# Layer 1's attention in a hybrid diffusion backbone: preparation of a pair of heads merged with the scores of the pair before, and a second bank for transposed scores

## The chip, the cores and the metric

The program runs on 1 core of one Trainium2 chip. The metric is the device time of one execution in microseconds (us), as the median of several. Instructions are written for five engines: TensorE (PE in the profile, its weight loads PEld), VectorE (DVE), ScalarE (ACT), GpSimd (POOL) and SyncE (SP, which issues the transfers). Each engine takes the instructions of its own queue in order.

## What is computed

The reference runs two layers over 512 latent tokens (`x`) and 256 context tokens (`ctx`), width 1024. In each layer one projection feeds three groups of heads whose outputs are put side by side and projected back:

- a bidirectional RWKV-7 scan (6 heads of 64),
- latent attention (6 heads; 64 values without and 32 with an axial rotation per head),
- an order-2 Hyena long convolution (256 channels).

Then comes a PEER feed-forward stage over 16384 single-neuron experts. Context tokens read context alone, latent tokens read latents and context. In the last layer only latents are wanted, so attention of the context there makes keys and values only. The part that is changed is this:

```python
q = rms_norm(q, q_gain)
k = rms_norm(k, k_gain)
...
q = concat([q[..., :64], apply_axial_rope(q[..., 64:], rope)])
k = concat([k[..., :64], apply_axial_rope(k[..., 64:], rope)])
...
s = einsum('bqhd,bkhd->bhqk', q, k) * (96 ** -0.5)
pr = softmax(s, axis=-1)
y = einsum('bhqk,bkhd->bqhd', pr, v)
```

## The kernel before

`layer0` (L484) and `layer1` (L540) hold the mixing stages; `ffn` (L1511) the PEER stages. Inside a mixing stage several generators run as tracks: the scan (`rwkv`, L779), Hyena (`hyena_filters` L1249, `hyena` L1338, and in layer 0 after it the modulation of layer 1, `mods` L386), and attention with the projections around it (`mla` L1105, `mixed` L735). Each generator yields numbers, its costs, and `weave` (L336) always goes on with the track whose sum is lowest; `scaled` multiplies a track's costs by a factor (0.42 for the scan in layer 0, 0.8 for that of the latents in layer 1, 0.05 for its context part there, 3.5 for the modulation, 1 for attention). A track that yields a condition (`after`) waits for a mark of another one. The order in which the instructions come out of the weave is their priority: the scheduler of the framework walks it with a model of the engines and puts on each engine's queue the earliest instruction whose inputs and buffers it thinks ready. `merge` (L848) is a small weave inside one track: it runs several generators side by side and yields on only what the slowest of them has advanced, so that two tracks of 46 and 22 units cost 46.

`mla` works for a stream b (0 context, 1 latents) with T tokens in nt tiles of 128. After the norms and V (L1145 to L1148) it goes over three pairs of heads, `g3`:

- Preparation. For keys (g = 1) and then queries (g = 0): products into "mm" (L1163, L1166), copies into `x` by ScalarE (L1164, L1167), squares and sums (L1175, L1176), a yield of 4, an inverse root on VectorE, the gain on GpSimd (L1181), the rotation on VectorE (L1190 to L1193), the scale on GpSimd (L1194), then per head nt transposes into "tr" (L1198), a copy into `kTl` or `qT` (L1200) and a yield of 2. A pair costs 2 x (4 + 2 x 2) = 16 units.
- Scores. Per head, for each tile of queries, products of the scores into "mm" and their maximum by VectorE (L1211); for latents 8 of them, then a yield of 5. The maxima go through "tr" into row 96 of `qT` (L1217, L1218), so that the next products are the transposed scores less the maximum. For each of 6 tiles of keys (2 for the context): the transposed scores into "tr" (L1223), the exponential into `PT` (L1225), the product with V into another "mm" bank (L1227), a yield of 2. Then the reciprocal of the sum (L1231), a wait for Hyena's mark, the product into the mixing tile `zl` (L1233), a yield of 1. A latent head costs 5 + 6 x 2 + 1 = 18 units.

`kTl` and `qT` have one buffer each, `PT` (shared with `sx`, `sq` and `rc`) three. PSUM has eight banks: `ps` (L274) gives two each for "mm", "rw" and "ch", one each for "tr" and "hy". Hyena uses "hy", the scan "rw" and "ch".

In layer 0 attention of the context comes first (78 units), then, once the scan of the context is done, its output projection (24), then attention of the latents, then, after the first mark of the modulation, `mixed` for the latents. The scan is 9 groups of at most 41 units and a last chain of 25, times 0.42: 165.5. In layer 1 attention begins with 27 units of projection for the context and 24 for its keys; the scan is 143 x 0.05 = 7 and then (6 x 41 + 25) x 0.8 = 217. `mixed(1, 1)` (L582) comes after the weave; its first step splits the eight mixing tiles (L748, L749), and the products need all of them.

## Time and profile before

| | us |
|---|---|
| median of 3 runs | 5449.75 |
| lowest and highest | 5433.88, 5454.05 |
| the profiled execution | 5464.84 |
| its span, first to last instruction | 5463.1 |
| TensorE busy | 4928.4 (90%) |
| VectorE busy | 3849.6 (70%) |
| ScalarE busy | 1918.5 (35%) |
| GpSimd busy | 1241.3 (23%) |

The profile is one execution. Times in the rows are microseconds from the start of the span. A busy TensorE is not one at its peak: matmuls overlap and their ends are modelled. L272 is the line of the helper that issues every matmul, so TensorE's rows are told apart by their tiles: `tr<-qT,kTl` are transposed scores, `mm<-PT,Vl` the product with V, `mm<-kTl,qT` the scores for the maxima, `ch<-...` and `rw<-...` the scan, `hy<-...` Hyena, `ch<-wl,silr` the modulation. A matmul of fp32 shows as two instructions.

### The profile page before, as it was taken

How to read it: one execution, taken by the hardware profiler on the slowest of the kernel's cores; microseconds unless marked ns; L12 is line 12 of the kernel's file. 1: busy time of each engine (PE TensorE's matmuls, PEld its weight loads, DVE VectorE, ACT ScalarE, POOL GpSimd, SP SyncE). 2: the span in 40 equal slices, each digit the busy share in tenths (PEclk: the TensorE clock that was granted, in tenths of full speed). 3: DMA queues.
4: the chain of work that ended last, by engine and by line, in shares of the span. 5: the costliest groups of instructions: out<-in, count | busy, mean ns of one | idle time of the engine just before them, and what ended most of it. 6: DMA issues, size and time to landing. Idle time of an engine off the chain costs nothing. (4 is left out here: it accounts for less than half of the span.)

```text
span 5463.1 us, 76042 instructions
## 1 busy us (share of the span) xinstructions
PE 4928.4 (90%) x28693; PEld 3745.5 (69%) x28693; DVE 3849.6 (70%) x8277; ACT 1918.5 (35%) x3438; POOL 1241.3 (23%) x933
## 2 busy tenths in 40 slices
PE   7987998889989999999999678888889889999998
PEld 4765676547644588887878456656657667888887
DVE  6356666656896488887888875656646985777776
ACT  5322222443254333333333232222223454444442
POOL 2322212221200122222222363211122321111110
PEclk9977899899999999999999889777899999999999
DMA  6300121342365788888888764200022668888885
GB/s 207 103 22 31 51 86 55 113 151 71 109 187 162 240 326 316 330 323 311 318 325 303 274 238 153 77 1 1 1 74 82 196 191 295 324 322 312 321 320 206
DMA packets 395517, 1028.18 MB, mean 188 GB/s; under 512 B 31780, under 2 KB 198981, under 8 KB 339597
## 3 DMA queue, kind: packets, MB, share of 16 engines
q1 hardware_dynamic: 339852, 620.65, 34.0%
q0 software_dynamic: 55296, 402.68, 19.6%
q8 instruction: 225, 3.69, 0.3%
q14 instruction: 144, 1.17, 0.1%
HBM read 920.19 MB, written 103.02 MB: 187 GB/s over the span
## 5 line engine op out<-in xcount | busy, mean ns | idle before, releaser
L203 POOL DMA_INDIRECT row<-in_uv,idx x384 | 531.8, 1385 | 1860.8 <-DVE acc L241 1586.7
L659 ACT ACTIVATE wh<-w 128x1024 fp32r<-128x1024 f32 (+1 forms) x557 | 571.0, 1027 | 1049.5 <-PE mm L272 461.7
L272 PE MATMUL mm<-hlo,wh 128*128 128x512 f32 (+2 forms) x2408 | 877.0, 368 | 30.7 <-DVE zl L688 7.5
L272 PE MATMUL mm<-hhi,wh 128*128 128x512 f32 (+2 forms) x2408 | 866.8, 364 | 0.0
L660 DVE TENSOR_TENSOR wl<-w,wh 128x1024 fp32r<-128x1024 f32 x424 | 516.3, 1221 | 255.0 <-ACT wh L659 252.1
L272 PE MATMUL mm<-hhi,wl 128*128 128x512 f32 (+2 forms) x2408 | 531.5, 361 | 1.7 <-POOL wl L660 1.7
L272 PEld LDWEIGHTS mm<-hlo,wh 128*128 128x128 f32 x2408 | 461.2, 192 | 104.4 <-issue 18.4
L241 DVE SCALAR_TENSOR_TENSOR acc<-row,act,acc 128x1024 f32<-128x1024 f32 x381 | 496.5, 1303 | 35.3 <-ACT act L237 34.6
L272 PEld LDWEIGHTS mm<-hhi,wh 128*128 128x128 f32 x2408 | 461.5, 192 | 61.8 <-issue 3.3
L219 DVE SCALAR_TENSOR_TENSOR row<-row,xk 128x1024 f32<-128x1024 f32 x384 | 480.3, 1251 | 16.5 <-DMA row<-in_uv,idx 16.3
L272 PE MATMUL mm<-row,wh 128*128 128x512 f32 (+1 forms) x1056 | 455.5, 574 | 29.9 <-DMA wh<-in_uT 25.1
L272 PEld LDWEIGHTS mm<-hhi,wl 128*128 128x128 f32 x2408 | 425.9, 189 | 56.6 <-issue 3.8
L660 POOL TENSOR_TENSOR wl<-w,wh 128x1024 fp32r<-128x1024 f32 (+1 forms) x133 | 291.4, 2198 | 670.0 <-ACT wh L659 405.3
L272 PEld LDWEIGHTS mm<-row,wh 128*128 128x128 f32 x1056 | 195.3, 195 | 211.2 <-issue 165.4
L236 ACT ACTIVATE act<-act 128x1 f32<-128x1 f32 x384 | 75.7, 197 | 498.6 <-DVE row L219 498.3
L1779 ACT ACTIVATE stage<-ch 128x512 f32<-128x512 f32 x224 | 218.2, 1101 | 62.6 <-PE ch L272 59.8
L1546 ACT ACTIVATE g<-mm 128x512 f32<-128x512 f32 (+1 forms) x256 | 137.6, 538 | 232.3 <-PE mm L272 197.2
L272 PE MATMUL rw<-wh,cl 128*128 128x512 f32 x512 | 201.5, 394 | 6.5 <-DVE cl L1614 3.5
L272 PE MATMUL rw<-wl,ch 128*128 128x512 f32 x512 | 200.5, 392 | 0.0
L272 PE MATMUL rw<-wh,ch 128*128 128x512 f32 x512 | 199.9, 390 | 0.0
L272 PE MATMUL ch<-wh,cl 128*128 128x512 f32 x512 | 199.6, 390 | 0.0
L272 PE MATMUL ch<-wh,ch 128*128 128x512 f32 x512 | 199.4, 389 | 0.0
(542 smaller groups left out, 10206.0 us busy)
## 6 DMA issues: line engine op xcount, KB each, us to landing
w<-in_uv SPq DMA_DIRECT2D x256, 512.0 KB
w<-in_uT SPq DMA_DIRECT2D x190, 512.0 KB
Wd<-stage SPq DMA_DIRECT2D x28, 2048.0 KB
w<-in_mod_w SPq DMA_DIRECT2D x192, 256.0 KB
wh<-in_uT SPq DMA_DIRECT2D x66, 512.0 KB
W<-Wd SPq DMA_DIRECT2D x32, 1024.0 KB
W<-Wd SPq DMA_DIRECT2D x32, 768.0 KB
w<-in_wq SPq DMA_DIRECT2D x32, 512.0 KB
```

The lines of the kernel that those rows point to most:

```text
L203: self.nc.gpsimd.indirect_dma_start(out=row, out_offset=None, in_=self.k.io[f"uv{self.li}"], in_offset=bass.IndirectOffsetOnAxis(ap=self.t ...
L219: nc.vector.scalar_tensor_tensor(row[:, 0:1024], row[:, 0:1024], 1.0, self.x, op0=OP.mult, op1=OP.mult, accum_out=act)
L236: nc.scalar.activation(act, act, AF.Gelu)
L241: nc.vector.scalar_tensor_tensor(self.acc, row[:, 1024:], act, self.acc, op0=OP.mult, op1=OP.add)
L272: self.nc.tensor.matmul(out, lhsT, rhs, start=start, stop=stop, skip_group_check=True)
L659: self.nc.scalar.activation(wh[:, s], w, AF.Copy)
L660: eng.tensor_tensor(wl[:, s], w, wh[:, s].bitcast(F32), op=OP.subtract)
L1546: nc.scalar.activation(g, p[:, 0:ND], AF.Gelu)
L1779: nc.scalar.activation(stage[:, :, u:u + 4].rearrange("p a t -> p t a"), p, AF.Copy, scale=1 / GS)
```

## The change

The body of the loop over pairs is cut into two generators, `prep(g3)` and `attend(g3)`. Before the loop `prep(0)` runs alone; then, for each pair, `attend(g3)` and `prep(g3 + 1)` run merged in layer 1, one after the other in layer 0. In layer 1 `kTl` and `qT` have two buffers. Every second tile of transposed scores goes into the bank "hy" instead of "tr", in either layer, if Hyena of the latents has set its last mark at that point of the program. There are new yields, in either layer: 3 after the scale on GpSimd; 4 after the second and the fourth tile of score maxima of a latent head; and 2 instead of 5 after the last. A latent pair's preparation so costs 22 units and a latent head 23; a context pair's preparation 22 (11 in layer 1, where only keys are made), a context head 5 as before.

```diff
-            for g3 in range(3):
+            def prep(g3):
+
                 if b:
-                    kTl = ap.tile([97, 2, T], F32, name="kTl")
+                    kTl = ap.tile([97, 2, T], F32, name="kTl", bufs=1 + li)
                     nc.gpsimd.memset(kTl[96:97], 1.0)
-                qT = ap.tile([97, 2, T], F32, name="qT") if full else None
+                qT = ap.tile([97, 2, T], F32, name="qT", bufs=1 + li) if full else None
+                made[g3] = kTl if b else None, qT
                 for g in (1, 0):
...
                     nc.gpsimd.tensor_tensor(x2, x2, r[:, :, None].to_broadcast([128, n, 96]), op=OP.mult)
+                    yield 3
                     for h in range(2):
...
                         yield 2
-                if not full:
-                    continue
+
+            def attend(g3):
+                kTl, qT = made[g3]
                 for h in range(2):
...
                             nc.vector.tensor_reduce(mx[:, i, z:z + 1], p, axis=AX.X, op=OP.max)
-                    yield 5 if b else 2
+                        if b and i % 2:
+                            yield 4
+                    yield 2
...
                     for n, kt in enumerate(kts):
-                        p = self.ps("tr")[:, :T]
+                        p = self.ps("hy" if n % 2 and ("hy", li, 1, 1) in self.marks else "tr")[:, :T]
...
                     yield 1
+
+            made = {}
+            yield from prep(0)
+            for g3 in range(3):
+                tracks = ([attend(g3)] if full else []) + ([prep(g3 + 1)] if g3 < 2 else [])
+                yield from self.merge(*tracks) if li else itertools.chain(*tracks)
```

## Rows read from the trace of the kernel before

**Rows 1.** The page, part 2: TensorE and its granted clock in 40 slices
```profile
PE   7987998889989999999999678888889889999998
...
PEclk9977899899999999999999889777899999999999
```

**Rows 2.** Windows: length, PE, PEld, DVE, ACT, POOL busy (instructions), PEclk, DMA share, GB/s
```profile
777.00:1042.00 265.00, 231.99 (x2338) 167.31 (x2336) 185.23 (x479) 78.43 (x155) 65.96 (x50) 0.88 0.22 73
1042.00:1195.00 153.00, 134.13 (x459) 60.12 (x459) 91.78 (x179) 74.74 (x138) 30.98 (x24) 0.90 0.40 121
...
3573.00:4033.00 460.00, 382.53 (x3740) 268.69 (x3738) 290.16 (x803) 123.09 (x246) 60.36 (x48) 0.80 0.01 1
4033.00:4061.00 28.00, 20.83 (x44) 8.40 (x44) 5.33 (x4) 6.69 (x10) 4.67 (x2) 0.74 0.23 75
```

**Rows 3.** Timeline of VectorE at layer 1's end: start, duration, instruction, idle before
```profile
4033.34 0.69 DVE L1102 TENSOR_TENSOR zl<-rw,g 128x512 f32<-128x512 f32 x1 [7.69 <-PE rw L272]
4036.41 0.69 DVE L749 TENSOR_TENSOR mlo<-zl,mhi 128x512 fp32r<-128x512 f32 x1 [2.38 <-ACT mhi L748]
...
4060.40 0.69 DVE L1233 TENSOR_TENSOR zl<-mm,rc 64x512 f32<-64x512 f32 x1
```

**Rows 4.** Timeline of TensorE there: steps of a head, first product of the projection
```profile
4011.37 1.12 PE L272 MATMUL mm<-PT,Vl 128*128 128x512 f32 x2 [0.31 <-ACT PT L1225]
4012.33 1.02 PE L272 MATMUL tr<-qT,kTc 97*128 97x512 f32 x2
4013.19 1.02 PE L272 MATMUL mm<-kTl,qT 96*128 96x512 f32 x2
...
4061.24 0.76 PE L272 MATMUL mm<-mlo,wh 128*128 128x512 f32 x1 [4.26 <-DVE zl L1233]
```

**Rows 5.** Timeline of VectorE at the end of layer 0's scan and of its attention
```profile
1036.45 0.41 DVE L1211 TENSOR_REDUCE mx<-mm 128x1 f32<-128x256 f32 x1
...
1042.09 0.69 DVE L1102 TENSOR_TENSOR zl<-rw,g 128x512 f32<-128x512 f32 x1 [3.11 <-PE rw L272]
...
1193.75 0.69 DVE L1233 TENSOR_TENSOR zl<-mm,rc 64x512 f32<-64x512 f32 x1
```

**Rows 6.** Timeline of ScalarE in layer 1: exponentials and copies into qT
```profile
3741.54 0.60 ACT L1225 ACTIVATE PT<-tr 128x512 f32<-128x512 f32 x1 [2.85 <-PE tr L272]
...
3785.37 0.68 ACT L1200 ACTIVATE qT<-tr,qkc 96x512 f32<-96x512 f32 x1 [1.63 <-PE tr L1198]
...
3906.88 0.60 ACT L1225 ACTIVATE PT<-tr 128x512 f32<-128x512 f32 x1
...
3975.66 0.67 ACT L1200 ACTIVATE qT<-tr,qkc 96x512 f32<-96x512 f32 x1
...
4052.47 0.60 ACT L1225 ACTIVATE PT<-tr 128x512 f32<-128x512 f32 x1 [2.14 <-PE tr L272]
4055.20 0.60 ACT L1225 ACTIVATE PT<-tr 128x512 f32<-128x512 f32 x1 [2.14 <-PE tr L272]
```

**Rows 7.** Timeline of ScalarE in layer 0 after the scan
```profile
1098.59 0.60 ACT L1225 ACTIVATE PT<-tr 128x512 f32<-128x512 f32 x1 [0.84 <-PE tr L272]
...
1129.70 0.68 ACT L1200 ACTIVATE qT<-tr,qkc 96x512 f32<-96x512 f32 x1 [0.58 <-PE tr L1198]
...
1155.69 0.60 ACT L1225 ACTIVATE PT<-tr 128x512 f32<-128x512 f32 x1 [1.22 <-PE tr L272]
1158.42 0.60 ACT L1225 ACTIVATE PT<-tr 128x512 f32<-128x512 f32 x1 [2.14 <-PE tr L272]
...
1187.09 0.60 ACT L1225 ACTIVATE PT<-tr 128x512 f32<-128x512 f32 x1 [1.15 <-PE tr L272]
```

**Rows 8.** Windows, tile tr, then tile mm: length, PE, PEld, DVE, ACT busy
```profile
1042.00:1195.00 153.00, 33.98 (x96) 14.28 (x96) 0.00 (x0) 19.38 (x32) 0.90 0.40 121
...
1042.00:1195.00 153.00, 60.70 (x143) 25.60 (x144) 32.31 (x38) 3.00 (x8) 0.90 0.40 121
```

## The prediction

> **What bounds the kernel now.** I read the page first. Its row of TensorE in 40 slices is nearly full, and shows where it is less so: eights in slices 7 to 9 and 25 to 30, the latter with sevens in the row of the granted clock [rows 1]. Those lie in the two mixing stages, of layer 0 and of layer 1, where attention, the RWKV scan and the Hyena convolution share the engines; the dense PEER stages between them are full and the change doesn't touch them. So I cut the mixing stages into windows. In layer 1 from 3573 (the first preparation of latent heads) to 4033 us, TensorE is busy for 382.5 of 460 us at a granted clock of 0.80, and in the last 28 us, to 4061, for 20.8 at 0.74; the DMA engines are idle. In layer 0, 777 to 1042 us is shared with the scan (232 of 265 busy) and 1042 to 1195 is attention beside the modulation of layer 1 (134 of 153) [rows 2]. Neither stage is full, none waits for memory: what ends last there is a chain.
>
> Which chain, the VectorE timeline tells. In layer 1 the scan's last output is written at 4033.3, the last head of attention at 4060.4, and between them VectorE does almost nothing [rows 3]. TensorE's first products of the output projection that need that head start at 4061.2, after 4.3 us of waiting for it [rows 4]. So attention ends layer 1's mixing, 27 us after everything else. In layer 0 it is the same, only more: the scan's last output is at 1042.1, the last head at 1193.8 [rows 5], and the projection follows at once. Attention's own length is therefore worth time in both layers, and the scan's length is worth time as the point from which attention stands alone.
>
> Attention's length has two visible parts. One is serial preparation: in layer 1 the last exponential of pair 0 is at 3741.5 and the last copy into qT of pair 1 at 3785.4, 44 us; from pair 1 to pair 2 it is 3906.9 to 3975.7, 69 us [rows 6]. The other is the single bank for transposed scores: at the end the exponentials come every 2.73 us, 0.60 of it work and 2.14 waiting for TensorE [rows 6], and in layer 0's lone stretch it is the same 2.73 [rows 7]. TensorE's share of such a step is one product of scores and one with V: 4011.37 to 4012.33 and 4012.33 to 4013.19, together 1.82 us [rows 4].
>
> **The change part by part.** No instruction is added or taken away, and no transfer, so SP's queue is passed by nothing; the extra buffers of kTl and qT in layer 1 are memory alone. What changes is order, and one bank.
>
> *Layer 1, preparation beside scores.* Preparation of pairs 1 and 2 leaves the chain, 44 and 69 us as it stands. That isn't the gain, because the scan goes on meanwhile: if attention stops being last, the scan's end at 4033.3 is, and the most that can be won with the scan unmoved is 4061.2 - 4037 (its copy and split of that tile follow in 4 us: the VectorE row at 4036.4 [rows 3]) = 24 us. Does attention get there? The yields are the clock by which the tracks are woven. Before, attention of layer 1 takes 27 + 24 units for the context and then 3 x (16 + 2 x 18) = 156, so it is due at 207; the scan is due at 7 + 0.8 x 271 = 224. Attention was due 17 units before the scan and came 27 us after it: it was late by its chain, not by its order. After, a preparation is 22 and a head 23 units, the context ends at 60, and the merge takes 22 + 3 x 46 = 160: due at 220, still before the scan. With the chain shorter by 113 us and the due time later by 13 of 217 scan units (13/217 of 460 us, 28 us), attention should come within some us of the scan. Against it stands work: the last head's products now run before 4033 instead of after. TensorE's 20.8 us of the last 28 [rows 2] have to fit into 77 idle us of the 460; I let 6 of them push the scan out. Sum -24 + 6 = **-18 us**; ends: 0 if attention is still last, and -40 if a denser order also moves the scan up (a fifth of those 77 idle us, an estimate).
>
> *Shared banks.* In the merge the next preparation draws on the bank "tr" and the two "mm" banks that the scores use, and the three PT buffers. Four transposed copies of 0.68 us a pair [rows 6] and their transposes sit between steps of the present pair. They cost attention's chain perhaps 4 x 2 us a pair; it has 113 us to give, so nothing, and 16 us if that cover is gone. The preparation's GpSimd work moves past the scan's in that queue, and GpSimd is busy for 60 of the 460 us [rows 2]: nothing. The second bank is Hyena's; in either layer its mark says that Hyena is done, so nobody queues behind it.
>
> *Layer 0, the yields.* Here the order within attention stays, but its clock doesn't: 156 units become 204, and the context's 78 become 96, because the new yields stand outside the test on the layer. The scan is due at 0.42 x 394 = 165.5 in both. Before, attention stands there at 165.5 - 102 = 63 of its 156 units: two heads done and most of preparation 1. After, at 165.5 - 120 = 45 of 204: one head. So one head and one preparation are moved behind the scan, where attention is alone. Alone a head takes 28.7 us (last exponential 1158.4 to 1187.1) and a preparation 31.8 (1098.6 to the end of 1129.7 + 0.68) [rows 7]: 60.5. The traced order runs ahead of the woven one (head 2's maxima are already being reduced at 1036 us [rows 5], due at 170 units and the scan's end at 165.5), so I take three quarters, +45. The scan gains what it no longer shares: attention's tiles take 34.0 + 60.7 = 94.7 us of TensorE for four heads and one preparation [rows 8]; counting a preparation as half a head, head and preparation are 32, three quarters of it 24, at 88% busy about -20 us. Ends: 0, if TensorE fills idle time with attention as before, and +45 with nothing moved up.
>
> *The second bank.* In layer 1 the Hyena mark is due at 60, before all six heads; in layer 0 at 164, after head 0, so for five heads. In layer 1 it helps to reach the bound that is taken above and counts once. In layer 0 each step may fall from 2.73 to 1.82: 0.9 x 5 steps x 5 heads = -22; I take **-17**, since the modulation's products stand in the same queue; ends 0 and -22. The Trainium skill, page "TensorE: Matmul & The Clock Gate", section "HAM oscillation — how this bites in real kernels", reports a kernel where adding PSUM double-buffering gave no further gain once its loop order was right. By that this term would be 0 and layer 0's sum +25; the 2.14 us of waiting before exponentials in this trace speak against it.
>
> *Layer 0's other queues.* The modulation now has its units before attention's end (318 against 324, before 318 against 258), so it comes earlier in every queue; TensorE's products for it already ran mostly before 1195. I cost it at nothing; if it takes precedence over attention it is in the end of +45.
>
> **Sum.** Layer 0: +45 - 20 - 17 = +8. Layer 1: -18. Together -10 us. The profiled execution is 5464.84 us for a span of 5463.1, 15 us over the median of 5449.75, itself within 5433.9 to 5454.1. Against the span 5453, against the median **5440 us**. About 27 us, 0.5%, is what a measurement of this kernel can tell from no change, and the forecast is inside it.
>
> **The rivals.**
> *A, layer 1 gives more.* Three tracks instead of two fill TensorE's gaps, the scan's end moves up too, and layer 0's order turns out to matter little because ready work is issued when the engine is free. Layer 1 -35, layer 0 between -10 and 0: about 5410. For it: 77 idle us and the clock of 0.80 in layer 1, which is a mean of stretches at 1.2 and at 2.4 GHz. Against it: the scan's own chain isn't shortened by anything.
> *B, slower.* Layer 0's attention is pushed behind the scan and stays there. Place: the stretch from the scan's last output to the last head, 152 us now. Price: +60 with -26 back from the scan, and nothing from the second bank, since steps are already interleaved with products of the modulation in TensorE's one queue; +34 in layer 0, -5 in layer 1: about 5479. It decides once more than a head's length is moved without the step falling below 2.5 us. The skill's sentence above is on its side; the trace, with 2.14 us of idle ScalarE a step, against it.
> *C, the change doesn't do what it says in layer 1.* Preparation and scores fight over "tr" and "mm"; attention still ends 20 us after the scan. Layer 1 0 to -5, layer 0 +8: about 5455.
>
> **How the numbers follow.** Forecast 0.50; A 0.26; B 0.14; C 0.10. Forecast and C lie within 27 us, A beyond it on the one side, B on the other: faster 0.26, same 0.60, slower 0.14. Range: from a little under A, 5400, to B, 5478; the forecast's own, with the ends of its terms, is 5415 to 5470.
>
> **What would show it.** Right in layer 1: the preparation's kTl and qT copies of the next pair lie between exponentials of the present one, exponentials come under 2.2 us apart at the end, and the last head is written within 10 us of the scan's last output. Right in layer 0: the scan's last output moves up by 10 to 30 us, the stretch from it to the last head grows from 152 us to 165 to 190, steps in it fall towards 2 us. The forecast is wrong if layer 0's stretch grows with the scan's end unmoved (B), or if the scan in layer 1 itself ends over 15 us sooner (A), or if attention is still over 15 us late there (C).

## The result: slower by half a per cent, and the profile after

The changed kernel takes **5490.4 us** (median of 8 runs, 5467.86 to 5505.14) against 5452.14 for the kernel before (8 runs, 5433.88 to 5470.19): ratio **1.0066 [1.0044, 1.0089]**. A second measurement, below, gives 1.0049 [1.0031, 1.0068]. The change is slower: by 38 us in the first measurement and by 27 in the second; 5440 was forecast.

The profiled execution took 5477.02 us, its span is 5475.3, only 12.2 over the one before, since the profiled execution before lies over its kernel's median (5464.84 against 5452.14) and this one under its own. Going by marks that both traces have, these 12.2 us are: +26.0 up to the first top-16 maximum (L1437 before, L1449 after) of layer 0's PEER stage (1286.3 to 1312.4); -12.5 in that stage, which the change doesn't touch (2150.4 to 2137.9 until layer 1's first Hyena output; in the profiles of this study it takes 2138 to 2165); -2.6 in layer 1's mixing (630.1 to 627.5 until its first projection output at L762); +1.3 behind it. By this profile the loss is layer 0's, and layer 1 gives nothing; runs of either layer alone, below, bear it out.

The page, part 2, of the changed kernel:

```profile
PE   7987898889988999999999778889889889999998
...
PEclk9976898899999999999999889867789999999999
```

Against [rows 1] the digits hardly move: layer 1's begin 7, 7, 8 for 6, 7, 8, with a 9 among its eights, over a clock that now shows a 6; slice 5, the end of the context's part in layer 0, has an 8 for a 9, and so has slice 13, outside both stages. No stage has become full, and none much emptier; digits are too coarse for half a per cent. The two stages in windows (columns as in [rows 2]); first layer 0 from its first values of the context (L1148) to the end of the context's scan and on to the first top-16 maximum, then its lone stretch, then layer 1:

```profile
319.00:616.00 297.00, 241.97 (x2027) 179.44 (x2027) 203.64 (x554) 76.40 (x161) 71.98 (x82) 0.72 0.11 36
616.00:1312.00 696.00, 609.68 (x4708) 402.49 (x4707) 427.07 (x1005) 232.87 (x432) 149.22 (x115) 0.89 0.28 90
...
1032.00:1222.00 190.00, 162.18 (x548) 75.28 (x546) 114.14 (x260) 89.58 (x169) 39.11 (x30) 0.87 0.35 107
3450.00:4078.00 628.00, 524.68 (x4849) 379.75 (x4849) 383.80 (x1054) 170.53 (x337) 99.03 (x81) 0.78 0.07 23
3582.00:4064.00 482.00, 410.30 (x3770) 286.69 (x3770) 293.84 (x820) 131.22 (x261) 59.31 (x47) 0.78 0.02 6
4051.00:4064.00 13.00, 5.05 (x24) 3.26 (x24) 3.52 (x12) 0.63 (x1) 3.78 (x3) 0.50 0.46 161
```

The same three stretches of the kernel before, which the prediction hadn't cut so:

```profile
318.00:609.00 291.00, 234.43 (x2011) 176.13 (x2010) 201.84 (x551) 73.81 (x159) 73.09 (x82) 0.74 0.10 33
609.00:1286.00 677.00, 602.17 (x4695) 396.86 (x4694) 428.06 (x1007) 230.96 (x430) 149.95 (x114) 0.90 0.29 94
...
3437.00:4067.00 630.00, 521.91 (x4841) 374.77 (x4838) 385.59 (x1052) 166.44 (x332) 94.72 (x80) 0.79 0.06 20
```

The first reading to take from them is length less TensorE's busy time, its **idle time**. In layer 1's stage it is 628 - 525 = 103 us, before 630 - 522 = 108. The 24 us at the end of layer 1 that were to be won stood in the trace, but only 5 us of TensorE's idle time have gone with them. The last row tells one reason: now the scan's end stands alone for 13 us, in which TensorE is busy for 5.05 at a granted clock of 0.50, where before attention's last 28 us had it busy for 20.8. In layer 0 behind the context's scan idle time is 86 us, before 75.

VectorE, timeline, the ends of scan (L1102) and attention (L1239; before L1233) in both layers:

```profile
1031.71 0.69 DVE L1102 TENSOR_TENSOR zl<-rw,g 128x512 f32<-128x512 f32 x1 [5.30 <-PE rw L272]
...
1221.13 0.69 DVE L1239 TENSOR_TENSOR zl<-mm,rc 64x512 f32<-64x512 f32 x1
...
4051.48 0.69 DVE L1239 TENSOR_TENSOR zl<-mm,rc 64x512 f32<-64x512 f32 x1
...
4064.18 0.69 DVE L1102 TENSOR_TENSOR zl<-rw,g 128x512 f32<-128x512 f32 x1 [9.39 <-PE rw L272]
```

In layer 0 the scan ends 10 us sooner than in [rows 5] and attention 27 us later: the lone stretch has grown from 152 to 189 us. In layer 1, against [rows 3], attention ends 9 us sooner and the scan 31 us later, in a stage that begins 14 us later (first Hyena output at 3450.3, before at 3436.7); they have changed places.

ScalarE, timeline: first layer 0's last two heads, then layer 1:

```profile
1176.93 0.60 ACT L1231 ACTIVATE PT<-tr 128x512 f32<-128x512 f32 x1
1178.97 0.60 ACT L1231 ACTIVATE PT<-hy 128x512 f32<-128x512 f32 x1 [1.44 <-PE hy L272]
...
1186.15 0.60 ACT L1231 ACTIVATE PT<-hy 128x512 f32<-128x512 f32 x1 [0.26 <-PE hy L272]
1204.22 0.59 ACT L1224 ACTIVATE qT<-tr 1x512 f32<-1x512 f32 x1 [1.04 <-PE tr L272]
...
3747.67 0.59 ACT L1231 ACTIVATE PT<-hy 128x512 f32<-128x512 f32 x1
3748.91 0.69 ACT L1203 ACTIVATE qT<-tr,qkc 96x512 f32<-96x512 f32 x1 [0.65 <-PE tr L1201]
```

The six exponentials of a lone head go from 1176.93 to 1186.15, five steps of 1.84 us where [rows 7] have 2.73. In layer 1 the copy into qT of the next pair (3748.91) follows an exponential of the present pair's first head: the merge does what it says. But from a head's last exponential to the row that opens the next (`qT<-tr` of one partition) 18.1 us pass. Before, its row stood 12.4 us behind the exponential at 1158.42 [rows 7] (ScalarE, timeline before):

```profile
1170.79 0.59 ACT L1218 ACTIVATE qT<-tr 1x512 f32<-1x512 f32 x1 [1.76 <-PE tr L272]
```

TensorE's timeline shows why. After:

```profile
1184.17 1.02 PE L272 MATMUL tr<-qT,kTc 97*128 97x512 f32 x2
1185.03 1.02 PE L272 MATMUL hy<-qT,kTc 97*128 97x512 f32 x2
1185.94 1.99 PE L272 MATMUL mm<-PT,Vc 128*128 128x512 f32 x4
1187.76 0.60 PE L272 MATMUL mm<-kTc,qT 96*128 96x256 f32 x2
```

Before, at the same place:

```profile
1154.57 1.02 PE L272 MATMUL tr<-qT,kTc 97*128 97x512 f32 x2
1155.43 1.02 PE L272 MATMUL mm<-kTl,qT 96*128 96x512 f32 x2
1156.34 1.12 PE L272 MATMUL mm<-PT,Vc 128*128 128x512 f32 x2
```

Before, a product of the next head's scores (`mm<-kTl,qT`) ran while ScalarE made its exponential. With two banks TensorE goes straight to the next transposed scores, and the next head's scores come after them. Products of the modulation are put off in the same way. ScalarE's wait of 2.14 us was no idle time of TensorE in this head.

### The profile page after: what moved, and what is told of

It reads as the page before. It is cut to its first block, busy times and chain, and to the rows that moved or that the text cites. A ratio compares the mean times of both kernels' runs of the same rounds, so it can differ in the third digit from the quotient of the medians.

```text
span 5475.3 us, 76056 instructions
## 1 busy us (share of the span) xinstructions
PE 4944.3 (90%) x28693; PEld 3759.4 (69%) x28693; DVE 3847.8 (70%) x8277; ACT 1924.1 (35%) x3440; POOL 1241.6 (23%) x933
## 5 line engine op out<-in xcount | busy, mean ns | idle before, releaser
L272 PEld LDWEIGHTS mm<-hlo,wh 128*128 128x128 f32 x2408 | 463.1, 192 | 103.5 <-ACT wh L659 13.6
```

The source lines that it names most:

```text
L272: self.nc.tensor.matmul(out, lhsT, rhs, start=start, stop=stop, skip_group_check=True)
```

## The experiments

Diffs are against the changed kernel, in terms of two constants, a flag for each layer, that switch the new yields and the second bank:

```diff
-                    yield 3
+                    if YIELDS[li]:
+                        yield 3
...
-                        if b and i % 2:
+                        if b and i % 2 and YIELDS[li]:
                             yield 4
-                    yield 2
+                    yield 2 if YIELDS[li] or not b else 5
...
-                        p = self.ps("hy" if n % 2 and ("hy", li, 1, 1) in self.marks else "tr")[:, :T]
+                        p = self.ps("hy" if n % 2 and BANKS[li] and ("hy", li, 1, 1) in self.marks else "tr")[:, :T]
```

"No merge" is, with one buffer each of `kTl` and `qT`:

```diff
-                yield from self.merge(*tracks) if li else itertools.chain(*tracks)
+                yield from itertools.chain(*tracks)
```

All results in one table, in us of each profile. Layer 0: **ctx** is from L1148's first value to the context's last scan output; **scan** from there to the latents' last scan output; **lone** from there to the last head; **idle** TensorE's from the end of ctx to the first top-16 maximum. Layer 1, from its first Hyena output: **scan** to the scan's last output, **head** the last head against that, **stage** to the first projection output, with **idle** of TensorE.

| kernel | ratio [95%] | ctx | scan | lone | idle | L1 scan | head | stage | idle |
|---|---|---|---|---|---|---|---|---|---|
| before | | 291 | 433 | 152 | 75 | 597 | +27 | 630 | 108 |
| after | 1.0066 [1.0044, 1.0089] | 297 | 416 | 189 | 86 | 614 | -13 | 627 | 103 |
| e5 (after) | 1.0049 [1.0031, 1.0068] | 299 | 416 | 189 | 85 | 620 | -13 | 634 | 103 |
| e1 | 1.0013 [0.9994, 1.0032] | 284 | 438 | 153 | 74 | 620 | -13 | 634 | 103 |
| e2 | 1.0024 [1.0011, 1.0037] | 296 | 413 | 189 | 87 | 603 | +27 | 638 | 108 |
| e3 | 1.0082 [1.0066, 1.0099] | 294 | 410 | 200 | 96 | 603 | +27 | 638 | 108 |
| e4 | 1.0004 [0.9987, 1.0021] | 277 | 448 | 142 | 74 | 593 | +27 | 628 | 107 |
| e9 | 1.0028 [1.0008, 1.0048] | 289 | 412 | 179 | 87 | 593 | +27 | 627 | 108 |
| e10 | 1.0044 [1.0027, 1.0060] | 273 | 445 | 162 | 83 | 593 | +27 | 626 | 108 |
| e11 | 1.0054 [1.0034, 1.0073] | 285 | 479 | 94 | 80 | 621 | -13 | 634 | 102 |
| e6 | 0.9986 [0.9971, 1.0000] | 268 | 435 | 152 | 75 | 604 | -13 | 617 | 105 |
| e13 (e6) | 0.9975 [0.9960, 0.9990] | 290 | 438 | 153 | 74 | 604 | -13 | 617 | 105 |
| e14 | 0.9990 [0.9962, 1.0017] | 281 | 444 | 154 | 76 | 604 | -13 | 617 | 106 |
| e15 | 0.9991 [0.9971, 1.0010] | 279 | 430 | 143 | 74 | 609 | -13 | 622 | 102 |
| e7 | 0.9996 [0.9979, 1.0013] | 280 | 445 | 153 | 77 | 618 | +1 | 631 | 96 |
| e8 | 1.0008 [0.9989, 1.0027] | 284 | 438 | 153 | 76 | 614 | -13 | 628 | 103 |
| e12 | 1.0026 [1.0006, 1.0045] | 268 | 438 | 153 | 74 | 615 | +24 | 645 | 104 |

Ratios rest on 5 to 12 executions of each kernel, the other columns on one profile each. Two things to see before the single runs. Kernels with the same layer 0 differ by up to 23 us in ctx (268 to 291), but by 2 us in "lone" and 3 in "idle": lengths carry the run's luck with the clock, idle time and the distance of two ends hardly do. And the change in layer 0 shows in every column.

### Which layer

**e1_layer1_alone**: layer 1 as after, layer 0 as before.

```diff
+YIELDS = (0, 1)
+BANKS = (0, 1)
```

> Layer 0 as before (its yields and its bank are kept), layer 1 as after. If the loss comes from layer 0's new yields: layer 0 as in the trace of before (scan's last output about 1042, last head about 1194, first PEER product about 1286), and the whole 5440 to 5455 us, ratio 0.998 to 1.001 to before, since layer 1's stage in the trace of after is 0 to 5 us shorter than in that of before. If the loss comes from layer 1 (the scan pushed out by attention's earlier work): 5475 to 5490 us, ratio 1.004 to 1.007.

Measured 1.0013 [0.9994, 1.0032], 5470.41 us against 5462.83. The whole of layer 1's change is worth nothing, or a little less. Its stage takes 634 us, as after (627 and 634).

**e2_layer0_alone**: layer 0 as after, layer 1 as before (no merge).

```diff
+YIELDS = (1, 0)
+BANKS = (1, 0)
```

> Layer 0 as after (new yields and second bank), layer 1 as before (old yields, one bank, one after the other, one buffer). If the loss is layer 0's: 5475 to 5490 us, ratio 1.004 to 1.007, last head of layer 0 at about 1221. If it is layer 1's: 5445 to 5460.

Measured 1.0024 [1.0011, 1.0037], 5484.49 us against 5462.83. Slower; the median is in the range told for a loss of layer 0 (5475 to 5490), the ratio below it (1.004 to 1.007). Its profile has layer 0 as after in every column, with 989 us from L1148 to the first top-16 maximum. The loss is layer 0's. 1.0013 and 1.0024 together make 1.0037, inside the interval of e5 and below that of the first measurement.

**e5_after_again**: the changed kernel itself, measured again.

> The changed kernel again, beside the runs that undo a part of it. If layer 0's yields are the whole loss: ratio 1.002 to 1.007 to before, last head of layer 0 at 1215 to 1225, layer 1's mixing (first Hyena output to first product of the projection) 625 to 640 us as in before. If layer 1 costs time too: over 1.007 and a layer 1 stage over 640.

Measured 1.0049 [1.0031, 1.0068], 5488.65 us against 5461.69.

### Layer 0: yields or bank

**e3_layer0_yields**: layer 0's new yields, nothing else (no merge).

```diff
+YIELDS = (1, 0)
+BANKS = (0, 0)
```

> As the run before, but without the second bank in layer 0: only the new yields of layer 0. If the second bank repays 17 us there, as was forecast, this is about 17 us slower than the run with both (stretch from the scan's last output to the last head over 205 us against 189). If the bank only reorders work that TensorE has anyway: within 6 us of the run with both, stretch 185 to 195.

Measured 1.0082 [1.0066, 1.0099], 5511.96 us, the slowest of all. The lone stretch is 200 us, 48 more than before, and lies between the two expectations (over 205, 185 to 195). The times decide between them: this kernel's median is 27 us over that of e2 (5484.49), which has the second bank beside the same yields.

**e4_layer0_bank**: layer 0's second bank alone.

```diff
+YIELDS = (0, 0)
+BANKS = (1, 0)
```

> Only the second bank in layer 0, everything else as before. If a step's 2.14 us of waiting on ScalarE is lost time: the stretch from the scan's last output to the last head falls from 152 to about 130 to 137 us and the whole to 5430 to 5437. If TensorE fills that time with the next head's score products and with the modulation: stretch 148 to 156, the whole 5445 to 5458.

Measured 1.0004 [0.9987, 1.0021], 5465.91 us. Its ScalarE in the lone stretch (in these kernels lines stand 2 or 3 lower):

```profile
1152.82 0.60 ACT L1234 ACTIVATE PT<-hy 128x512 f32<-128x512 f32 x1 [0.26 <-PE hy L274]
1171.10 0.59 ACT L1227 ACTIVATE qT<-tr 1x512 f32<-1x512 f32 x1 [1.27 <-PE tr L274]
1173.40 0.60 ACT L1234 ACTIVATE PT<-tr 128x512 f32<-128x512 f32 x1
...
1182.40 0.60 ACT L1234 ACTIVATE PT<-hy 128x512 f32<-128x512 f32 x1 [2.14 <-PE hy L274]
```

Steps of (1182.40 - 1173.40)/5 = 1.80 us, and 18.3 us between heads, without any new yield: what a head gains in its steps goes, for the most part, to the scores of the next. The lone stretch falls by 10 us, to 142, between what was told for lost time (130 to 137) and for none (148 to 156), but the scan of the latents takes 448 us, and TensorE's idle time behind the context's scan is 74 as before. With the new yields the bank does repay something: from e3 to e2 idle falls from 96 to 87 us and the ratio from 1.0082 to 1.0024.

**e9_layer0_context_yield**: of all, only the yield of 3 in the context's preparation in layer 0 (no bank, no merge).

```diff
-                    yield 3
+                    if li == 0 and b == 0:
+                        yield 3
```

> Of all new yields only the 3 in the preparation of layer 0's context stream is kept (78 units become 96); all else as before. If the place of the context's output projection in the weave is what counts: that projection spreads from about 95 to 130 us or more, the first keys of the latents come 30 to 55 us later, the first PEER product of layer 0 is 10 to 25 us later than in before, ratio 1.002 to 1.005. If only the latents' own yields count (the forecast's step): first keys of the latents 10 to 20 us later, ratio under 1.002.

Measured 1.0028 [1.0008, 1.0048], 5477.04 us, as told for the projection's place in the weave. **e10_layer0_latent_yields**: only those of the latents in layer 0.

```diff
-                    yield 3
+                    if YIELDS[li] and b:
+                        yield 3
```

> Only the new yields of layer 0's latent stream (156 units become 204); all else as before. If the forecast's step is right: the scan's last output 5 to 20 us sooner, the stretch to the last head 175 to 195 us against 152, first PEER product 15 to 30 us later, ratio 1.003 to 1.006. If the context's yields carry the loss: stretch under 165, ratio under 1.002.

Measured 1.0044 [1.0027, 1.0060], 5481.12 us: the ratio is the one told for the forecast's step, but the lone stretch of 162 us is the one told against it (under 165), and the scan ends no sooner (1041.1 us, before 1042.1). The two make 1.0072, e3 measured 1.0082: the yields cost, each half by itself, and the ratios add. So does idle time: 75 before, 87 with the context's yield, 83 with those of the latents; 12 + 8 = 20, and e3 has 96. What is moved doesn't add: the lone stretch grows by 27 us in e9 and by 10 in e10, in e3 by 48; with either half two heads are done at the scan's end, as before, with both only one. The eight outputs of the context's projection (L762; 764 in e9 and e10), as the view of one line's instructions on VectorE shows them (first and last start), tell what the context's yield does. Before, then after:

```profile
L762 DVE SCALAR_TENSOR_TENSOR x<-mm,modc,x x8: 477/484/486, 663.7 to 758.1; 128x256 f32<-128x256 f32 x8
```

```profile
L762 DVE SCALAR_TENSOR_TENSOR x<-mm,modc,x x8: 475/484/484, 644.9 to 809.6; 128x256 f32<-128x256 f32 x8
```

With the context's yield alone (e9), then with the latents' alone (e10):

```profile
L764 DVE SCALAR_TENSOR_TENSOR x<-mm,modc,x x8: 473/479/484, 639.0 to 799.4; 128x256 f32<-128x256 f32 x8
```

```profile
L764 DVE SCALAR_TENSOR_TENSOR x<-mm,modc,x x8: 474/483/486, 648.5 to 745.0; 128x256 f32<-128x256 f32 x8
```

Attention of the context costs 96 instead of 78 units, so what follows on the same track comes later in the weave than the scan: its projection is spread over 165 us instead of 94, and attention of the latents, behind it, starts 50 us later (first copy into `kTl` at 858, before at 807).

**e11_layer0_earlier**: the other direction. Layer 0 as before, its attention's costs times 0.8; layer 1 with the second bank alone.

```diff
+YIELDS = (0, 0)
+BANKS = (0, 1)
-                yield from self.mla(0, 1, [zl[:, m] for m in range(17, 21)], yml, "right")
+                yield from self.scaled(self.mla(0, 1, [zl[:, m] for m in range(17, 21)], yml, "right"), 0.8)
```

(and the same for the context's).

> The other direction: attention of both streams of layer 0 woven at 0.8 of its old cost (context 62 units, latents 125), with the second bank in layer 1 alone; all else as before. If attention's place in the weave sets layer 0's end in both directions: stretch from the scan's last output to the last head 115 to 135 us, first PEER product 5 to 20 us sooner, ratio 0.994 to 0.997. If what is moved ahead only delays the scan by as much: first PEER product within 6 us of before, and the ratio that of the second bank in layer 1 alone, 0.997 to 1.000.

Measured 1.0054 [1.0034, 1.0073], 5486.68 us: a miss, neither expectation came. The lone stretch falls from 152 to 94 us, further than told, and the kernel is as slow as the changed one: the scan of the latents takes 479 us, 41 more than in e13, whose layer 0 is as before. A long lone stretch isn't the loss in itself; attention and scan share one engine, and here the other lost no less than the one gained. Idle time tells little of this loss: it is 80 us for 75, while the stretch from the context's scan to the first top-16 maximum takes 704 us, 686 in the mean of the eight profiles with layer 0 as before.

### Layer 1: merge or bank

**e6_layer1_bank**: the second bank in layer 1 alone (no merge).

```diff
+YIELDS = (0, 0)
+BANKS = (0, 1)
```

> Only the second bank in layer 1, everything else as before. If the last head's steps are lost time at the end (2.73 to 1.8 us apart, six of them, after the scan): attention ends 5 to 10 us sooner, the whole 5 to 10 us shorter, ratio 0.998 to 0.999. If TensorE's queue is what counts: within 4 us of before.

Measured 0.9986 [0.9971, 1.0000], 5452.24 us against 5461.69. The time is the one told for lost steps, but attention ends 40 us sooner against the scan, not 5 to 10. **e7_layer1_merge**: merge, buffers and yields in layer 1, no second bank.

```diff
+YIELDS = (0, 1)
+BANKS = (0, 0)
```

> Layer 1's merge, buffers and yields without the second bank; layer 0 as before. If the stage in layer 1 is a conserved amount of TensorE work that the merge only deals out differently: attention's last head 4045 to 4062, the scan's last output later than in before by 10 to 30 us, the stage within 8 us of before, ratio 0.998 to 1.003. If the merge needs the bank: attention ends over 15 us after the scan, ratio over 1.003. If preparation was the chain that counts (the forecast): 15 to 20 us shorter, ratio 0.996 to 0.997.

Measured 0.9996 [0.9979, 1.0013], 5463.08 us, with the scan later by 22 us and the stage within 1 us of before, as told for a conserved amount of work. The merge has the lowest idle time of all, 96 us, and its stage is 631 us: what ran, ran longer (busy 535 us against 522).

**e8_layer1_scan_first**: e1 with the scan of the latents woven at 0.7 of its cost.

```diff
-RC1, RL1 = 0.05, 0.8
+RC1, RL1 = 0.05, 0.7
```

> Layer 1 as after, layer 0 as before, and the scan of layer 1 woven at 0.7 instead of 0.8 (due at 197 units, attention at 220). If what was lost in layer 1 is that attention's work was dealt out ahead of the scan's: the scan's last output comes 8 to 20 us sooner than with 0.8, attention's last head later by less, and the stage is 5 to 12 us shorter than with 0.8, ratio to before 0.996 to 0.999. If the sum of TensorE's work alone counts: the ends change places and the stage stays within 4 us, ratio 1.000 to 1.003.

Measured 1.0008 [0.9989, 1.0027], 5472.52 us: a miss, and an explained one. In the traces the instructions of layer 1 stand in the same order on TensorE, VectorE, ScalarE and GpSimd as in e1 (compared by their tiles, in order of start): the factor changed no instruction's place, so the scan is still last by 13 us. That ready work, not the units, sets this order is the likely reading; no run shows it.

**e12_layer1_merge_old_yields**: merge, buffers and second bank in layer 1, old yields.

```diff
+YIELDS = (0, 0)
+BANKS = (0, 1)
```

> Layer 1 with merge, two buffers and second bank, but with the old yields (a preparation 16 units beside two heads of 36: due at 175 instead of 220); layer 0 as before. If layer 1's stage is a conserved amount of TensorE work, attention ends still further ahead of the scan (last head 25 to 50 us before the scan's last output) and the stage stays within 6 us of that of before, ratio 0.999 to 1.002. If the new yields in layer 1 held the merge back: stage 10 to 20 us shorter, ratio 0.996 to 0.998.

Measured 1.0026 [1.0006, 1.0045], 5471.52 us: a miss too. With fewer units attention was to end far ahead of the scan; its VectorE shows it 24 us behind:

```profile
4034.22 0.69 DVE L1104 TENSOR_TENSOR zl<-rw,g 128x512 f32<-128x512 f32 x1 [4.43 <-PE rw L274]
4058.41 0.69 DVE L1242 TENSOR_TENSOR zl<-mm,rc 64x512 f32<-64x512 f32 x1
```

Due times don't say here which track ends last. The scan was still pushed, to 615 us behind the first Hyena output. Every kernel with the merge has it at 614 to 620, those with layer 1 as before at 593 to 603, e6 at 604 and e11, with the layer 1 of e6, at 621. Whether e6's gain is real, from one profile that was its fastest execution, was to be settled, and whether it is the merge that pushes the scan. Three more runs:

**e13_layer1_bank_again** is e6.

> The same kernel as e6_layer1_bank: only layer 1's second bank. Theory (the bank alone takes attention off the end of layer 1, and without the merge the scan is pushed by under 10 us): from layer 1's first Hyena output to the scan's last output 598 to 607 us (before 593 to 603, with the merge 614 to 621), the last head before the scan's end, the stage to the first projection output 612 to 624 us, ratio 0.997 to 0.9995. Rival (the one profile of e6 was a lucky execution): the scan's end at 612 or more, the stage 627 to 636, ratio 0.9995 to 1.002.

Measured **0.9975 [0.9960, 0.9990]**, 5449.72 us against 5460.76: faster than both kernels. Stage and ends of layer 1 in its profile are those of e6, 617 and 604:

```profile
3446.00:4063.00 617.00, 511.57 (x4845) 367.07 (x4842) 387.36 (x1052) 169.85 (x334) 97.47 (x81) 0.79 0.07 23
```

```profile
4037.19 0.69 DVE L1242 TENSOR_TENSOR zl<-mm,rc 64x512 f32<-64x512 f32 x1
...
4049.87 0.69 DVE L1104 TENSOR_TENSOR zl<-rw,g 128x512 f32<-128x512 f32 x1 [9.39 <-PE rw L274]
```

The first is the window of the stage, the second VectorE's timeline at its end. Attention is 13 us ahead of the scan with one bank more and nothing else.

**e14_layer1_bank_yields** adds the new yields, without the merge.

```diff
+YIELDS = (0, 1)
+BANKS = (0, 1)
```

> Layer 1's second bank and its new yields, no merge, one buffer each of kTl and qT; layer 0 as before. Theory (the merge pushes the scan, not the yields): the scan's end 598 to 609 us after the first Hyena output, the stage 612 to 626 us, ratio 0.997 to 1.0005. Rival (the yields push it): the scan's end at 614 or more and the stage 628 to 640, ratio 1.000 to 1.003. Second rival: attention is due later by its longer units and is last again, the last head over 15 us after the scan's end.

Measured 0.9990 [0.9962, 1.0017], 5457.07 us; scan 604, stage 617, as in e13. But this run tells less than it was meant to: without the merge the yields leave layer 1's order on all four engines as in e13, as far as the records go, so it is e13 a third time, and the yields can't be told from the merge by it.

**e15_both_banks**: the second bank in both layers, nothing else.

```diff
+YIELDS = (0, 0)
+BANKS = (1, 1)
```

> Second bank in both layers, nothing else of the change. Theory (in layer 0 the bank takes from the lone stretch what it gives to the scan's end): layer 0 as in e4_layer0_bank, the stretch near 142 us, idle time of TensorE there unchanged (74 us from the context's scan to the first top-16 maximum), layer 1 as in e13; ratio within 0.001 of e13's, 0.997 to 1.000. Rival (with layer 1's bank beside it layer 0's counts): ratio 0.994 to 0.997.

Measured 0.9991 [0.9971, 1.0010], 5448.4 us: not the further gain of the rival. Layer 0 is as in e4, lone stretch 143, idle 74. Its ratio is 0.0016 from e13's, a little more than expected, with intervals that overlap.

The orders of layer 1 in the traces fall into groups, and make better samples than single kernels do. With layer 1 as before (before, e2, e3, e4, e9, e10) the stage is 626 to 638 us, 631 in the mean. With the second bank alone (e6, e13, e14, e15, and e11, in all of which layer 1 has one order) it is 617, 617, 617, 622 and 634, 621 in the mean; e11's 634 comes at a granted clock of 0.76, the others' at 0.77 to 0.80. With the change (after, e5, e1, e8) it is 627 to 634, 631 in the mean. So the bank alone is worth about 10 us in the profiles, 0.9975 to 0.9990 in the three timed runs of that order beside layer 0 as before, and one of the three intervals ends clearly below 1. By lengths alone it isn't sure, since e11's 634 is the bank's own order.

That the merge takes the gain back doesn't rest on these lengths. e8, whose layer 1 has the changed kernel's order, and e6 were timed on one chip, twelve runs each: medians 5472.52 and 5452.24 us, means 20 us apart (95% interval 10 to 31). And the intervals of e12 and e13, merge and bank against bank alone with the old yields, lie apart: [1.0006, 1.0045] and [0.9960, 0.9990]. The second buffers came with the merge in all of them and weren't tried by themselves.

Where the time goes can be added up. The granted clock in these traces has two levels, 2.4 and 1.2 GHz. Count the part of TensorE's busy time that lies at the lower one half, and busy times that differ by 30 us become nearly one sum: 405 to 412 us for layer 1's stage in all seventeen profiles (and 538 to 543 in layer 0 from the context's scan to the first top-16 maximum). A stage's length is this sum, plus idle time, plus half of the busy time at the lower level:

| layer 1 in us | stage | sum | idle | busy at 1.2 GHz |
|---|---|---|---|---|
| before | 630 | 412 | 108 | 220 |
| after | 627 | 406 | 103 | 237 |
| e5, e1 | 634 | 405 | 103 | 253 |
| e7 | 631 | 409 | 96 | 252 |
| e12 | 645 | 408 | 104 | 265 |
| e6, e13 | 617 | 411 | 105 | 202 |
| e15 | 622 | 409 | 102 | 221 |
| e11 | 634 | 408 | 102 | 248 |

Idle time differs by 12 us at most; the rest is how much of the same work ran at the lower clock. With the merge that is 237 to 265 us, with the bank alone 200 to 221, but 248 in e11.

## Why the prediction was wrong

**What bounds the kernel.** That attention ends both stages was read rightly. That its lateness is worth time was right only where TensorE was idle meanwhile, and the prediction had the number at hand: TensorE busy for 20.8 of the last 28 us [rows 2]. Two smaller readings were wrong: the DMA engines aren't idle in those 28 us (share 0.23, 75 GB/s [rows 2]), and the last head's six exponentials, from 4037.89 to 4055.20, come every 3.46 us in the mean; 2.73 are the last steps alone.

**Layer 1, forecast -18, measured about 0.** Failed step: "I let 6 of them push the scan out". The first half of the sum held: the first projection output stood 33.5 to 35 us behind the scan's end in the profiles with layer 1 as before, and 13.6 after, so about 20 of the 24 us were won. But the scan's end moved from 593 to 603 us behind the first Hyena output (mean 597 of before, e2, e3, e4, e9, e10) to 614 to 620 (mean 617 of after, e1, e5 and e8): pushed by 20, not 6. The windows show it as one account: TensorE's 382.5 + 20.8 = 403.3 us of before [rows 2] are 410.3 in the window from 3582 to 4064 after, at a clock of 0.78 for 0.80 and 0.74. The idle us that were to take up the last head's products did so in part: from the first preparation of latent heads to the later of the two ends idle time falls from 85 to 72 us. But the scan's end, now alone, has idle time of its own, and of the whole stage's 108 only 5 have gone; half of the 17 us more at the lower clock, 8 us, is added. With the second bank alone the sum of -24 and +6 comes nearly so in e6, e13 and e14: the scan pushed by 7, the stage 14 us shorter; in e15 and e11, with the same order, it is pushed by 12 and 24. What the merge adds is an earlier start of the later pairs, and one bank is enough to bring attention ahead of the scan; the timed runs show that it costs. How isn't settled: with the merge TensorE's idle time is 96 to 104 us, no more than with the bank alone (102 to 106), but it is busy for 524 to 541 us where e6, e13 and e14 have 511 or 512, at a granted clock of 0.77 or 0.78 against 0.79 or 0.80. e15 and e11, with the bank's order, have 519 and 532 at 0.77 and 0.76, so no profile shows that it is the merge which lowers the clock.

**Layer 0, forecast +8, measured +26.** (Means from L1148 to the first top-16 maximum: 966 us in the eight profiles with layer 0 as before, 949 to 977; 992 in after, e2 and e5, 989 to 995.) Of the 26 us 16 lie in the context's own stage (281 to 297 in the same profiles) and 10 behind it (686 to 695), where TensorE's idle time rises from 75 to 86. This accounts for the 27 us of the second measurement; what made it 38 in the first is not known. Term by term:

- One head and one preparation behind the scan, +45: in e3, which has the yields without the bank, the lone stretch grows by 48. Right, and so was the order: at the scan's end one head is done instead of two. The cause was named by half: the context's yield alone makes 27 of it (e9), the latents' alone 10 (e10).
- The scan's repayment, -20: from the context's scan to the latents' 438.7 us (mean of the eight) becomes 415. Right, -24; it comes with the context's yield (412 in e9) and not with the latents' (445 in e10).
- The second bank, -17: with the yields -10 in the lone stretch (e3's 199.6 to 189.2), of which the scan, 413 to 416 for 410, takes some back, and 27 us between the medians of e3 and e2; without the yields it is 0 (e4, 1.0004). So the size is about right for the changed kernel and the reason given for it isn't: a step was shortened by 0.9 us, as worked out, by putting off the next head's scores.
- The context's yield: the step that failed. The prediction counted its units, "the context's 78 become 96", only as a later place of the latents within +45, and gave them no term of their own. e9 shows that they cost by themselves (1.0028). In the profiles they show twice. The context's own stage is 289 to 299 us long in the five kernels that have the yield and 268 to 291 in the eleven others but e11, 280 in the mean against 295, at nearly the same idle time (after 55 us, before 57) and a lower granted clock (0.72 to 0.75 against 0.74 to 0.83). And behind it TensorE is idle for 87 instead of 75 us (e9), while the projection is drawn out. The ranges of the first overlap at 289 to 291, so the +15 is likely rather than sure, and why the clock is lower stays open; of the idle time, every kernel with the yield has at least 85 us and every one that has neither new yields nor e11's factor 74 to 77.
- The modulation, "I cost it at nothing; if it takes precedence over attention it is in the end of +45": it came earlier, its last group is done at 1215 us, before at 1269, but that this costs isn't shown. In a lone preparation TensorE waits over 3 us for its weights twice, 4.62 and 4.28 us, but it did so before too, 3.88 and 4.28 us. TensorE's timeline, the first of these waits after, then before:

```profile
1138.79 0.40 PE L272 MATMUL ch<-wl,silr 128*4 128x512 f32 x1 [4.62 <-DVE wl L404]
```

```profile
1109.98 0.59 PE L272 MATMUL ch<-wl,silr 128*4 128x512 f32 x1 [3.88 <-DVE wl L404]
```

This preparation, from the last exponential at 1126.92 to the end of the last copy into qT, begun at 1165.48, takes 39 us where it took 31.8 [rows 7]; TensorE's idle time in it is 13.0 us for 11.3, and 30 instructions of the modulation lie in either.

**The rivals.** B was the case that came: its place, the lone stretch of layer 0, and its price in that layer, +34, are nearer to what was measured than the forecast's +8. Its point of decision was wrong: the step did fall, to 1.84 us, and the kernel is slower all the same. The Trainium skill, page "TensorE: Matmul & The Clock Gate", section "HAM oscillation — how this bites in real kernels", reports a kernel where PSUM double-buffering gave no further gain. Layer 0's bank alone agrees with it (1.0004), layer 1's (0.9975) doesn't. That the difference is what TensorE had to run in the freed time, the modulation in layer 0, is argued, not shown. A is refuted: the scan's end doesn't move up in layer 1. C's 20 us of lateness is refuted too, but its price for layer 1, 0 to -5, is right.

**The signs to look for.** In layer 1 two of three came nearly as told: copies between exponentials, and the last head 13 us from the scan's last output (10 was written); the time didn't follow, since that output itself had moved. The third didn't: the last head's exponentials are 2.74 us apart in the mean, not under 2.2 (ScalarE's timeline after):

```profile
4030.78 0.60 ACT L1231 ACTIVATE PT<-tr 128x512 f32<-128x512 f32 x1 [1.22 <-PE tr L272]
...
4044.50 0.58 ACT L1231 ACTIVATE PT<-hy 128x512 f32<-128x512 f32 x1
```

In layer 0 the scan's end moved up by 10 us (10 to 30 written), the stretch grew to 189 (165 to 190), steps fell to 1.84. Most local signs were right; those that were missing are TensorE's idle time over the stage and the clock at which the rest ran.

## What to carry to other kernels

Where tracks share one engine, price a wait by that engine's idle time in the stage, not by the wait of the engine behind it: a step that is shortened for one track moves work to another. Idle time is the first of two terms: in layer 0 behind the context's scan it rises by 11 us where the changed kernel's length rises by 10; in e11 and in layer 1 it doesn't follow the length, and what is left there is how much of the same work ran at the lower clock. Costs that set a weave are part of the code: a yield that is meant for one layer and stands outside its test is a change of order in the other. Take the smallest part of a change that moves the end of the stage, here one bank, and measure it alone.

## What was not expected

Executions of one program differ by more than the change in stages that it doesn't touch: the context's stage of layer 0 took 268 to 291 us with the same instructions, at granted clocks of 0.83 and 0.74, with TensorE idle for 57 to 59 us in each. Idle time repeated within 3 us where lengths differed by 23, and TensorE's busy time did so within 3% once its part at the lower clock was counted half. And units and factors of the weave can be without effect: 0.7 for 0.8 on the scan left every instruction of layer 1 in its place, and so did the new yields without the merge.
